# Ordering edges on VectorE for two kinds of side work in the second half: dots of the best entries' rows, and the batched heads' first selection

## The chip, the cores and the metric

The kernel runs on one core of a Trainium2 chip. The metric is device time in microseconds (us) of one launch, as the median of several runs. Each of the core's engines runs its own instructions strictly in order: TensorE (PE, matrix multiply; PEld is its weight load), VectorE (DVE), ScalarE (ACT), GpSimd (POOL), and SyncE (SP), which here only issues transfers. An instruction waits for what it reads, and all behind it on its engine wait with it.

## The reference, cut to what matters

One decoder block over 1024 tokens of width 1024: two mixers (a gated linear attention, GLA, and a chunked spatial gating) share one input projection and one output projection; then comes PEER, a mixer that retrieves, per token and head, 16 of 16384 single-neuron experts.

```python
h = modulate(rms_norm(x, norm1_w[l]), shift1, scale1)
proj = jnp.einsum('btd,de->bte', h, w_in[l])
q, k, v, r, a_lr, su, sv, g_a, g_b = jnp.split(proj, IN_SPLITS, axis=-1)
...
y = jnp.einsum('bte,ed->btd', merged, w_out[l])
x = x + gate1[:, None, :] * y
h2 = modulate(rms_norm(x, norm2_w[l]), shift2, scale2)
y2 = peer(h2, peer_w_q[l], peer_keys1[l], peer_keys2[l], peer_down[l], peer_up[l])
...
# in peer, 8 heads, K = 16: per token
v1, i1 = lax.top_k(s1, K)
v2, i2 = lax.top_k(s2, K)
cand = (v1[..., :, None] + v2[..., None, :]).reshape(B, T, H, K * K)
top_s, pos = lax.top_k(cand, K)
g = jax.nn.softmax(top_s, axis=-1).astype(h.dtype)
# per block of 128 tokens
u = expert_down[ii]
a = jax.nn.gelu(jnp.einsum('pd,ped->pe', xx, u), approximate=False)
vv = expert_up[ii]
return jnp.einsum('pe,ped->pd', gg * a, vv)
```

## The kernel before

**Halves and weights.** The tokens are worked in two halves of 512 (four blocks of 128). Each half streams 184 weight tiles of 128x512 from HBM: eight k-tiles for each of the groups V0, V1, QK0, QK1, SV0, SV1 and so on, then the output projection and PEER's query projection. `weights_ahead` (L1353) brings each tile in: a transfer on SP into `wt` (L1358, four buffers), ACT makes the high part `wh` (L1362), DVE subtracts to get the low part `wl` (L1364, four buffers each). It keeps three weights ahead of the matmuls. A buffer of `wt` is free for the next transfer once the subtract L1364 of the weight four back is done. The matmuls run as three passes, high by high, high by low, low by high (L182, L183, L185 in `mm3s`; L188 to L190 for the first or last k-tile). Their sums stand in four PSUM banks `mm`, so a group's first matmul waits until the group before has been taken out of its bank. For QK0 this is done by DVE: L1493 and L1494 make `qs` and `q1` from the first bank, again from the second, then L1510 to L1512 make `kk` and `kt` from the third and fourth. The matmuls of QK1 follow.

**Side work.** While the second half's weights stream, the PEER work of the first half's tokens runs beside it. After each k-tile `step()` lets a few generators go on; among them:

- `route` chooses the experts of a token; the heads whose best 8 candidates per side weren't enough are batched up and go through `rare` (L391): indices on DVE (L395 to L427), a gather of the scores on POOL into `qsc` (L429), then the first selection, `tops16` (L204) for both sides: MAX (L205), MAX_INDEX (L206), MATCH_REPLACE (L207), and the next eight (L208, L209), then the selection among sums (`select16`).
- `direct_rows` (L740) adds the best entry of each head for each token of blocks 0 to 3: 32 entries of 128 rows. For each, POOL gathers two tiles `uvd` of 128x1024 (L753: first the rows u of `down`, then the rows v of `up`), DVE forms the dot product of u with `h2` (L765), ACT takes Gelu (L767), DVE multiplies by the gate (L768) and adds v times the result to `yd` (L774; the first of a block is written by ACT, L770). The `uvd` tiles go round in 8 buffers that hold four entries, so an entry's gathers wait for the dot or the addition of an earlier entry. Gathers are issued one entry ahead of the dot in the text of the program.

**What sets the order.** The kernel is written as generators, but a scheduler with a model of times puts each engine's instructions in order. `tc.issue_after(x)` adds an edge to it: what stands inside may come only behind instruction `x` on the same engine. It makes no semaphore. Such edges exist before the change (Gelu behind `zlast`, `wh` and `wl` behind `hlast`). All lines in this text are those of the kernel before; in the changed kernel they stand one or two higher from L436 on.

Of the kernel before, what the change touches and what calls it, by code (L numbers as in the profile page):

```python
# [7 lines left out]
F32 = mybir.dt.float32  # L8
# [4 lines left out]
OP = mybir.AluOpType  # L13
# [68 lines left out]
def block_kernel(ctx: ExitStack, tc: tile.TileContext, x, xT, cT, w_ada, b_ada, b_adaT, n1T, w_inp, w_alr,  # L82
                 w_al, b_alT, gla_w, ln_w, ln_b, wsT, sgu_bT, w_outp, n2_w, w_qp, keysT, tab, down, up, fin_w,
                 out, dbg=None):
    nc = tc.nc
# [49 lines left out]
    sc = const.tile([P, KD], F32, name="sc")  # L135
# [68 lines left out]
    def tops16(v, ix, st):  # L204
        nc.vector.max(v[:, 0:8], st)  # L205
        nc.vector.max_index(ix[:, 0:8], v[:, 0:8], st)  # L206
        nc.vector.match_replace(st, v[:, 0:8], st, NEG)  # L207
        nc.vector.max(v[:, 8:16], st)  # L208
        nc.vector.max_index(ix[:, 8:16], v[:, 8:16], st)  # L209
# [181 lines left out]
    def rare(gi, rps):  # L391
# [25 lines left out]
        r = r2.tile([P, 4], F32, name="qr")  # L417
# [14 lines left out]
        yield  # L432
        tv = r2.tile([P, 1, 2, TOPK], F32, name="qtv")
        ti = r2.tile([P, 1, 2, TOPK], U32, name="qti")
        for c in range(2):
            tops16(tv[:, 0, c], ti[:, 0, c], sc[:, c])  # L436
        yield
        ts, sel = yield from select16(r2, tv, ti, 1, "q")
        tsel = r2.tile([P, 3 * TOPK + 2], F32, name="qtsel")
# [295 lines left out]
        while b not in done:  # L735
            qr.pump()

    zlast = []

    def direct_rows(t4, bs):  # L740
        todo = [(b, h) for b in bs for h in range(PH)]
# [16 lines left out]
        for k, (b, h) in enumerate(todo):  # L758
            lists(k + 1)
            await_routing((b // BH, h // 2), weighted)  # L760
            if h == 0:
                y = rowp.tile([P, D], F32, name="yd", tag="row")
            u, v = ents.pop(k)
            r = r2.tile([P, 2], F32, name="rdr", bufs=4)
            nc.vector.scalar_tensor_tensor(u, u, 1.0, h2s[b], op0=OP.mult, op1=OP.mult, accum_out=r[:, 0:1])  # L765
            with tc.issue_after(zlast[0]):
                nc.scalar.activation(r[:, 1:2], r[:, 0:1], AF.Gelu)  # L767
            nc.vector.tensor_tensor(r[:, 1:2], r[:, 1:2], dcol(dgtq, b, h), op=OP.mult)  # L768
            if h == 0 and YA:
                nc.scalar.activation(y, v, AF.Identity, scale=r[:, 1:2])  # L770
            elif h == 0:
                nc.vector.tensor_scalar(y, v, r[:, 1:2], None, op0=OP.mult)
            else:
                nc.vector.scalar_tensor_tensor(y, v, r[:, 1:2], y, op0=OP.mult, op1=OP.add)  # L774
            if h == PH - 1:
                nc.scalar.dma_start(y_d[b], y)
                summed.add(b)
            yield
# [275 lines left out]
    with ExitStack() as pa:  # L1054
# [299 lines left out]
        def weights_ahead(n):  # L1354
            while plan and len(made) < n:
# [5 lines left out]
                with tc.issue_after(hlast[0]):  # L1361
                    nc.scalar.activation(wh, wt, AF.Identity)  # L1362
                with tc.issue_after(hlast[1]):
                    nc.vector.tensor_tensor(wl, wt, wh.bitcast(F32), op=OP.subtract)  # L1364
                made.append((wh, wl))

        for hf in range(NHALF):
# [505 lines left out]
```

## Time and profile before

| what | us |
| --- | --- |
| runs (3) | 1446.89, 1449.89, 1451.12; median 1449.89 |
| profiled execution, own time | 1451.39 |
| its span on the core | 1449.7 |
| PE busy in the span | 1354.9 |
| DVE busy | 1091.3 |
| ACT busy | 731.4 |
| POOL busy | 282.8 |

The profiled execution's time is 1.69 us longer than its span (work around the program), and 1.5 us above the median of the runs. In the views below, times are from the start of the span. "x <- y" behind an engine's wait names what released it: an engine, a tile and a line. A row of the timeline gives the start, the duration, the engine, the line, the operation, output<-inputs with shapes, and in brackets the idle time of the engine ahead of it. An inferred releaser is the one that came last in the profile.

### The profile page before, as it was taken

What the parts mean: (1) busy time and instruction counts of PE and PEld (TensorE: products, weight loads), DVE (VectorE), ACT (ScalarE), POOL (GpSimd) and SP (SyncE); (2) the same over time, 40 slices, a digit from 0 to 9 for tenths busy, and PEclk for the clock granted to TensorE, in tenths of its full rate; (3) what the DMA queues carried; (4) which work ended last, traced back from release to release, by engine and by line L of the source; (5) the groups of instructions that cost most, each with busy time, mean ns of one, the idle gap of its engine ahead of it and who ended that gap; (6) DMA issues with size and microseconds to landing.
All of it is one profiled execution on the core that took longest, in us unless ns stands there. A gap on an engine that the chain in (4) does not pass through costs nothing.

```text
span 1449.7 us, 19609 instructions
## 1 busy us (share of the span) xinstructions
PE 1354.9 (93%) x5998; PEld 1039.5 (72%) x5998; DVE 1091.3 (75%) x3105; ACT 731.4 (50%) x1603; POOL 282.8 (20%) x276
## 2 busy tenths in 40 slices
PE   7999999999998989997989999999988999789996
PEld 5578777888887878776767777787767876445553
DVE  5784767434478669989879787777799786799775
ACT  3463333333355456465444676556656555556542
POOL 0100001000000111332342123220111033444331
PEclk9999999999999999998999999999999999999999
DMA  8753544332257575856687689796688669998984
GB/s 277 276 195 114 183 154 132 109 102 80 95 197 257 185 282 167 294 181 244 203 281 261 210 318 341 276 354 217 221 314 292 225 215 335 314 375 352 418 299 175
DMA packets 120980, 345.00 MB, mean 238 GB/s; under 512 B 15049, under 2 KB 24521, under 8 KB 108962
## 3 DMA queue, kind: packets, MB, share of 16 engines
q0 software_dynamic: 32208, 165.95, 31.5%
q1 hardware_dynamic: 71600, 133.43, 27.5%
q10 hardware_dynamic: 17058, 44.29, 8.4%
q8 instruction: 48, 0.79, 0.2%
q14 instruction: 66, 0.54, 0.1%
HBM read 319.40 MB, written 24.23 MB: 237 GB/s over the span
## 4 chain that ended last, share of the span: by engine, by line
PE 35%; DMA 10%; DVE 9%; issue 6%; ACT 5%; POOL 2%; ACTq 0%; SPq 0%; DVEq 0%; POOLq 0%
PE acc L607 6%; PE mm L182 5%; PE mm L183 5%; PE mm L185 5%; DMA uv<-in_tab_dram,ix 2%; PE mm L188 2%; PE mm L190 2%; PE mm L189 2%; PE aux L1766 1%; DMA uvd<-in_down_dram,dix 1%; PE hps L579 1%; DMA uv<-in_tab_dram,dix 1%; DVE uv L581 1%; DVE wl L1364 1%; PE hps L580 1%
## 5 line engine op out<-in xcount | busy, mean ns | idle before, releaser
L1362 ACT ACTIVATE wh<-wt 128x512 fp32r<-128x512 f32 x360 | 223.2, 628 | 306.7 <-PE mm L183 118.2
L1364 DVE TENSOR_TENSOR wl<-wt,wh 128x512 fp32r<-128x512 f32 x360 | 241.4, 683 | 142.4 <-ACT wh L1362 70.5
L182 PE MATMUL mm<-wh,hTh 128*128 128x512 f32 x648 | 257.0, 397 | 4.1 <-ACT wh L1362 4.1
L183 PE MATMUL mm<-wh,hTl 128*128 128x512 f32 x648 | 254.4, 393 | 0.0
L185 PE MATMUL mm<-wl,hTh 128*128 128x512 f32 x648 | 202.9, 396 | 0.3 <-DVE wl L1364 0.2
L182 PEld LDWEIGHTS mm<-wh,hTh 128*128 128x128 f32 x648 | 122.0, 188 | 34.0 <-ACT wh L1362 6.0
L183 PEld LDWEIGHTS mm<-wh,hTl 128*128 128x128 f32 x648 | 121.9, 188 | 26.0 <-issue 1.0
L185 PEld LDWEIGHTS mm<-wl,hTh 128*128 128x128 f32 x648 | 120.9, 188 | 27.0 <-issue 1.1
L526 POOL DMA_INDIRECT uv<-in_tab_dram,ix x73 | 77.2, 1058 | 241.2 <-ACT ix L558 145.2
L182 PE MATMUL mm<-hTh,wh 128*128 128x512 f32 x240 | 96.9, 404 | 0.0
L183 PE MATMUL mm<-hTl,wh 128*128 128x512 f32 x240 | 95.8, 399 | 0.0
L188 PE MATMUL mm<-wh,hTh 128*128 128x512 f32 x216 | 86.1, 410 | 4.0 <-ACT sg L1598 2.8
L189 PE MATMUL mm<-wl,hTh 128*128 128x512 f32 x216 | 85.7, 397 | 0.0
L581 DVE SCALAR_TENSOR_TENSOR uv<-uv,hps 128x512 f32<-128x512 f32 x110 | 73.8, 680 | 15.6 <-PE hps L580 5.7
L190 PE MATMUL mm<-wh,hTl 128*128 128x512 f32 x216 | 85.4, 396 | 0.0
L188 PE MATMUL mm<-hTh,wh 128*128 128x256 f32 (+1 forms) x208 | 70.7, 343 | 11.5 <-DVE q L1494 7.3
L185 PE MATMUL mm<-hTh,wl 128*128 128x512 f32 x240 | 71.1, 398 | 0.0
L189 PE MATMUL mm<-hTl,wh 128*128 128x256 f32 (+1 forms) x208 | 69.0, 334 | 1.8 <-DVE hTl L174 1.8
L753 POOL DMA_INDIRECT uvd<-in_down_dram,dix x32 | 36.2, 1132 | 173.2 <-DMA wt<-in_w_qp_dram 38.8
L190 PE MATMUL mm<-hTh,wl 128*128 128x256 f32 (+1 forms) x208 | 67.9, 335 | 1.7 <-DVE wl L1364 1.7
L619 DVE SCALAR_TENSOR_TENSOR vl<-uv,r,vh 128x512 fp32r<-128x512 f32 x82 | 60.0, 745 | 10.5 <-ACT vh L618 6.8
L579 PE MATMUL hps<-hh,E 128*128 128x512 f32 x132 | 62.0, 470 | 4.4 <-DVE uvu L581 2.4
(967 smaller groups left out, 2939.4 us busy)
## 6 DMA issues: line engine op xcount, KB each, us to landing
wt<-in_w_inp_dram SPq DMA_DIRECT2D x224, 256.0 KB
wt<-in_w_qp_dram SPq DMA_DIRECT2D x80, 256.0 KB
wada<-in_w_ada_dram SPq DMA_DIRECT2D x32, 512.0 KB
wt<-in_w_outp_dram SPq DMA_DIRECT2D x64, 256.0 KB
wada<-in_w_ada_dram SPq DMA_DIRECT2D x32, 256.0 KB
s_d<-so ACTq DMA_DIRECT2D x28, 256.0 KB
xr<-in_x_dram ACTq DMA_DIRECT2D x8, 512.0 KB
x_d<-x ACTq DMA_DIRECT2D x8, 512.0 KB
```

The lines of the kernel that those rows point to most:

```text
L182: nc.tensor.matmul(ps, lh, rh, start=False, stop=False)
L183: nc.tensor.matmul(ps, *((lh, rl) if feat else (ll, rh)), start=False, stop=False)
L185: nc.tensor.matmul(ps, *((ll, rh) if feat else (lh, rl)), start=False, stop=False)
L188: nc.tensor.matmul(ps, lh, rh, start=first, stop=False)
L189: nc.tensor.matmul(ps, lh, rl, start=False, stop=False)
L190: return nc.tensor.matmul(ps, ll, rh, start=False, stop=last).ins
L526: nc.gpsimd.indirect_dma_start(out=dst[:], out_offset=None, in_=src, in_offset=off)
L579: nc.tensor.matmul(hps, Ej, hh[:, sl], start=True, stop=False)
L581: nc.vector.scalar_tensor_tensor(uv[0][:, sl], uv[0][:, sl], 1.0, hps, op0=OP.mult, op1=OP.mult, accum_out=r[:, 2 + n:3 + n])
L607: ins = nc.tensor.matmul(acc[:, sl], W, v[:, sl], start=first, stop=last).ins
L1362: nc.scalar.activation(wh, wt, AF.Identity)
L1364: nc.vector.tensor_tensor(wl, wt, wh.bitcast(F32), op=OP.subtract)
```

## The change

Three places and one list. The last low-part subtract written so far is remembered in `last_wl`; the dots of `direct_rows` (L765) and the first selection of `rare` (L435, L436) get an edge behind it. No instruction is added or removed; their counts are the same on every engine, as are ACT's 68 table loads. The second group's selection (second half's tokens) comes after the last weight, where the edge says nothing.

```diff
--- before.py
+++ after.py
@@ -432,8 +432,9 @@
         yield
         tv = r2.tile([P, 1, 2, TOPK], F32, name="qtv")
         ti = r2.tile([P, 1, 2, TOPK], U32, name="qti")
-        for c in range(2):
-            tops16(tv[:, 0, c], ti[:, 0, c], sc[:, c])
+        with tc.issue_after(last_wl[0]):
+            for c in range(2):
+                tops16(tv[:, 0, c], ti[:, 0, c], sc[:, c])
         yield
         ts, sel = yield from select16(r2, tv, ti, 1, "q")
         tsel = r2.tile([P, 3 * TOPK + 2], F32, name="qtsel")
@@ -735,7 +736,7 @@
         while b not in done:
             qr.pump()
 
-    zlast = []
+    zlast, last_wl = [], []
 
     def direct_rows(t4, bs):
         todo = [(b, h) for b in bs for h in range(PH)]
@@ -762,7 +763,8 @@
                 y = rowp.tile([P, D], F32, name="yd", tag="row")
             u, v = ents.pop(k)
             r = r2.tile([P, 2], F32, name="rdr", bufs=4)
-            nc.vector.scalar_tensor_tensor(u, u, 1.0, h2s[b], op0=OP.mult, op1=OP.mult, accum_out=r[:, 0:1])
+            with tc.issue_after(last_wl[0]):
+                nc.vector.scalar_tensor_tensor(u, u, 1.0, h2s[b], op0=OP.mult, op1=OP.mult, accum_out=r[:, 0:1])
             with tc.issue_after(zlast[0]):
                 nc.scalar.activation(r[:, 1:2], r[:, 0:1], AF.Gelu)
             nc.vector.tensor_tensor(r[:, 1:2], r[:, 1:2], dcol(dgtq, b, h), op=OP.mult)
@@ -1361,7 +1363,7 @@
                 with tc.issue_after(hlast[0]):
                     nc.scalar.activation(wh, wt, AF.Identity)
                 with tc.issue_after(hlast[1]):
-                    nc.vector.tensor_tensor(wl, wt, wh.bitcast(F32), op=OP.subtract)
+                    last_wl[:] = [nc.vector.tensor_tensor(wl, wt, wh.bitcast(F32), op=OP.subtract).ins]
                 made.append((wh, wl))
 
         for hf in range(NHALF):
```

What it does to the order: the first nine dots of `direct_rows` stand 4 to 19 weights later than before on DVE (the first behind the 181st subtract L1364 in place of the 163rd, the ninth behind the 194th in place of the 189th); the tenth to the fifteenth stand where they were or one or two weights later, and from the sixteenth on the places are the same, counted so. On POOL the two MEMSETs of `smask` move ahead of the gathers of two entries, and the gather of `qsc` moves behind one more gather of `up`. PE's order is the same up to the end of QK1 but for one set of matmuls; further on, the second half's matmuls and PEER's accumulations are interleaved differently in many places.

The first place is DVE at the end of QK0 of the second half, where `qsc` is first read. `wl_5937` is the low part of QK1's first weight (the 201st subtract L1364), `uvd_5898` and the `yd` rows belong to the direct entries. Before:

```order
L774 SCALAR_TENSOR_TENSOR yd_5736<-uvd_5734,rdr_5769,yd_5736 128x1024
L425 CAST qr_5532<-rtok0_127 128x1
L768 TENSOR_TENSOR rdr_5929<-rdr_5929,dgt0_2_141 128x1
L205 MAX qtv_5573<-qsc_5544 128x8 x2
L1364 TENSOR_TENSOR wl_5937<-wt_5934,wh_5936 128x512
L774 SCALAR_TENSOR_TENSOR yd_5736<-uvd_5767,rdr_5857,yd_5736 128x1024
L427 TENSOR_SCALAR rcol0_129<-qr_5532 128x1 x4
```

The changed kernel at the same weight:

```order
L767 SCALAR_TENSOR_TENSOR uvd_5898,rdr_5929<-uvd_5898,h2d_5674 128x1024
L424 TENSOR_SCALAR rtok0_127<-qix_5536 128x1
L1366 TENSOR_TENSOR wl_5937<-wt_5934,wh_5936 128x512
L776 SCALAR_TENSOR_TENSOR yd_5736<-uvd_5734,rdr_5769,yd_5736 128x1024
L770 TENSOR_TENSOR rdr_5902<-rdr_5902,dgt0_1_140 128x1
L425 CAST qr_5532<-rtok0_127 128x1
L770 TENSOR_TENSOR rdr_5929<-rdr_5929,dgt0_2_141 128x1
L776 SCALAR_TENSOR_TENSOR yd_5736<-uvd_5767,rdr_5857,yd_5736 128x1024
L427 TENSOR_SCALAR rcol0_129<-qr_5532 128x1 x4
```

The MAX on `qsc` no longer stands ahead of the weight's low part, and neither does the first `yd`, which is now behind it; the dot of entry 12 (`uvd_5898`), which stood ahead of the 200th weight's low part, stands behind that one and directly ahead of this one.

The second place is DVE directly behind it: the next weight's low part `wl_5955` (the 202nd), and the rows that empty QK0's banks (L1493 to L1512 before; `qs`, `q1`, `kk`, `kt`). Before:

```order
L206 MAX_INDEX qti_5574<-qtv_5573,qsc_5544 128x8
L765 SCALAR_TENSOR_TENSOR uvd_5925,rdr_5974<-uvd_5925,h2d_5674 128x1024
L206 MAX_INDEX qti_5574<-qtv_5573,qsc_5544 128x8
L226 TENSOR_TENSOR candq_5585<-qtv_5573 128x24
L226 TENSOR_TENSOR candq_5585<-qtv_5573 128x16
L1364 TENSOR_TENSOR wl_5955<-wt_5952,wh_5954 128x512
L774 SCALAR_TENSOR_TENSOR yd_5736<-uvd_5855,rdr_5902,yd_5736 128x1024
L207 MATCH_REPLACE qsc_5544<-qtv_5573,qsc_5544 128x128
L765 SCALAR_TENSOR_TENSOR uvd_5970,rdr_6001<-uvd_5970,h2d_5674 128x1024
L1493 SCALAR_TENSOR_TENSOR qs_6008<-mm_5798,eG_6006 128x4x64
L1494 SCALAR_TENSOR_TENSOR q1_6009<-mm_5798,eG_6006 128x256
L1493 SCALAR_TENSOR_TENSOR qs_6015<-mm_5799,eG_6013 128x4x64
```

The changed kernel:

```order
L1366 TENSOR_TENSOR wl_5955<-wt_5952,wh_5954 128x512
L767 SCALAR_TENSOR_TENSOR uvd_5925,rdr_5974<-uvd_5925,h2d_5674 128x1024
L1495 SCALAR_TENSOR_TENSOR qs_6008<-mm_5798,eG_6006 128x4x64
L1496 SCALAR_TENSOR_TENSOR q1_6009<-mm_5798,eG_6006 128x256
L776 SCALAR_TENSOR_TENSOR yd_5736<-uvd_5855,rdr_5902,yd_5736 128x1024
L1495 SCALAR_TENSOR_TENSOR qs_6015<-mm_5799,eG_6013 128x4x64
L1496 SCALAR_TENSOR_TENSOR q1_6016<-mm_5799,eG_6013 128x256
L1512 TENSOR_TENSOR kk_6020<-mm_5800,eGi_6024 128x4x2x64
L1513 TENSOR_TENSOR kk_6020<-mm_5800,dt_6022 128x4x64
L1514 TENSOR_TENSOR kt_6021<-mm_5800,dt_6022 128x4x64
L205 MAX qtv_5573<-qsc_5544 128x8 x2
L1366 TENSOR_TENSOR wl_5982<-wt_5979,wh_5981 128x512
```

The two MAX_INDEX, the two sums `candq`, one MATCH_REPLACE and one dot (`uvd_5970`) that stood ahead of the first `qs` are now behind the third bank's `kt`; one `yd` now stands between the first bank and the second.

The third place is ACT some 15 us earlier, at `eG`, `eGi` and `dt` (the decays of QK0) and the high parts `wh_5824` (the 197th weight) and `wh_5864`. Before:

```order
L1488 ACTIVATE eG_6006<-G0_5435 128x512
L1488 ACTIVATE eG_6013<-G1_5443 128x512
L770 ACTIVATE yd_5736<-uvd_5678,rdr_5737 128x1024
L1552 ACTIVATE egl3_5795<-G3_5459 128x4x2
L1507 ACTIVATE eGi_6024<-G0_5435 128x512
L1508 ACTIVATE dt_6022<-dt_6022 128x512
L1508 ACTIVATE dt_6033<-dt_6033 128x512
L1362 ACTIVATE wh_5824<-wt_5822 128x512
L1362 ACTIVATE wh_5864<-wt_5862 128x512
```

The changed kernel:

```order
L1490 ACTIVATE eG_6006<-G0_5435 128x512
L1490 ACTIVATE eG_6013<-G1_5443 128x512
L769 ACT_TABLE_LOAD
L769 ACTIVATE rdr_5737<-rdr_5737 128x1
L1554 ACT_TABLE_LOAD
L1554 ACTIVATE egl3_5795<-G3_5459 128x4x2
L1509 ACTIVATE eGi_6024<-G0_5435 128x512
L1510 ACTIVATE dt_6022<-dt_6022 128x512
L1364 ACTIVATE wh_5824<-wt_5822 128x512
L1510 ACTIVATE dt_6033<-dt_6033 128x512
L772 ACTIVATE yd_5736<-uvd_5678,rdr_5737 128x1024
L1364 ACTIVATE wh_5864<-wt_5862 128x512
```

The Gelu of entry 8 (`rdr_5737`), which stood higher with three others, is now between two table loads of its own ahead of `egl3`, and `yd_5736`, the first of a block, moves behind `wh_5824`.

## The prediction

> **What bounds the kernel now.** The page's first part says which engine to follow:
>
> ```profile
> PE 1354.9 (93%) x5998; PEld 1039.5 (72%) x5998; DVE 1091.3 (75%) x3105; ACT 731.4 (50%) x1603; POOL 282.8 (20%) x276
> ```
>
> PE is busy for 93% of the span, so DVE's order is worth only what it adds to or takes from PE's gaps. The dots run from 518 to 763 us (the group of their line gives 32 of them, quoted below), so next come the windows of that stretch. A row has the engines' busy us in the order PE, PEld, DVE, ACT, POOL, then the granted clock, the DMA share and GB/s.
>
> ```profile
> 550.00:575.00 25.00, 25.00 (x125) 20.20 (x124) 24.70 (x101) 16.33 (x29) 1.00 (x1) 1.00 0.37 126
> 575.00:600.00 25.00, 25.00 (x126) 20.71 (x125) 25.00 (x136) 13.06 (x23) 7.88 (x8) 1.00 0.72 232
> 600.00:625.00 25.00, 25.00 (x107) 17.95 (x106) 17.62 (x54) 13.46 (x23) 8.12 (x8) 1.00 0.75 268
> 650.00:675.00 25.00, 17.74 (x79) 14.43 (x78) 23.70 (x64) 12.28 (x21) 5.96 (x5) 0.80 0.74 265
> 725.00:750.00 25.00, 19.75 (x85) 15.89 (x84) 16.57 (x30) 9.06 (x26) 11.06 (x11) 0.86 0.92 325
> ```
>
> From 550 to 600 DVE is full, but PE is full too: nothing is to be won there. From 600 to 625 DVE has 7.4 us to spare. PE loses time in two windows, 7.3 us after 650 and 5.3 us after 725, both with a lower clock. PE's waits, asked for in 640 to 680 and in 725 to 760, give one row each (line waited for: us in total, times, longest):
>
> ```profile
> PE mm L188 <- DVE q L1494: 7.3, 1, 7.3
> PE gaux L1537 <- DVE rdr L768: 5.3, 1, 5.3
> ```
>
> The first is the change's target: QK1's first matmul waits for QK0's first bank. The timeline shows what DVE did ahead of it:
>
> ```profile
> 640.45 1.27 DVE L774 SCALAR_TENSOR_TENSOR yd<-uvd,rdr,yd 128x1024 f32<-128x1024 f32 x1
> 641.65 0.68 DVE L1364 TENSOR_TENSOR wl<-wt,wh 128x512 fp32r<-128x512 f32 x1
> ...
> 651.30 0.49 DVE L205 MAX8 qtv<-qsc 128x8 f32<-128x128 f32 x2 [3.26 <-DMA qsc<-s_d,qix]
> 651.79 0.69 DVE L1364 TENSOR_TENSOR wl<-wt,wh 128x512 fp32r<-128x512 f32 x1
> ...
> 653.84 0.08 DVE L206 MATCH_VALUE_LOAD qti<-qtv,qsc 128x8 f32 x1
> ...
> 654.11 1.21 DVE L765 SCALAR_TENSOR_TENSOR uvd<-uvd,h2d 128x1024 f32<-128x1024 f32 x1
> 655.24 0.08 DVE L765 DVE_READ_ACCUMULATOR uvd<-uvd,h2d 128x1 f32 x1
> ...
> 655.68 0.68 DVE L1364 TENSOR_TENSOR wl<-wt,wh 128x512 fp32r<-128x512 f32 x1
> 656.29 1.28 DVE L774 SCALAR_TENSOR_TENSOR yd<-uvd,rdr,yd 128x1024 f32<-128x1024 f32 x1
> 657.48 0.08 DVE L207 MATCH_VALUE_LOAD qsc<-qtv,qsc 128x8 f32 x1
> ...
> 657.75 1.21 DVE L765 SCALAR_TENSOR_TENSOR uvd<-uvd,h2d 128x1024 f32<-128x1024 f32 x1
> 658.89 0.42 DVE L1493 SCALAR_TENSOR_TENSOR qs<-mm,eG 128x256 f32<-128x256 f32 x1
> 659.22 0.41 DVE L1494 SCALAR_TENSOR_TENSOR q<-mm,eG 128x256 f32<-128x256 f32 x1
> ```
>
> DVE stood idle for 3.26 us at MAX, and then had 7.6 us of work (651.30 to 658.89) ahead of the first `qs`, while PE had run out. But the idle time is not MAX's alone: the weight behind it was late too, as ACT, SP and PE show.
>
> ```profile
> 642.35 14.38 SPq L1358 DMA_DIRECT2D wt<-in_w_inp_dram  x6
> 651.13 0.63 ACT L1362 ACTIVATE wh<-wt 128x512 fp32r<-128x512 f32 x1 [4.85 <-DMA wt<-in_w_inp_dram]
> 652.13 0.39 PE L190 MATMUL mm<-hTh,wl 128*128 128x512 f32 x1
> 659.78 0.77 PE L188 MATMUL mm<-hTh,wh 128*128 128x512 f32 x1 [7.26 <-DVE q L1494]
> ```
>
> The transfer of weight 201 was issued at 642.35, as soon as the subtract at 641.65 had freed its buffer, and landed 8.8 us later; its high part was ready at 651.76, its subtract could not start before 651.8. So **taking MAX out of the way frees no 3.26 us**: in the changed order that subtract still stands ahead of the banks, and DVE waits there for ACT instead.
>
> **The change part by part.**
>
> *Taken from ahead of the first bank* (second place in the order): by differences of starts, the first MAX_INDEX 0.27 us (653.84 to 654.11), the second with both sums 0.44 (655.24 to 655.68), MATCH_REPLACE 0.27 (657.48 to 657.75), one dot 1.14 (657.75 to 658.89): 2.12 us. The two `yd` ahead of the bank stay two, since one comes from above the subtract and one goes below. Two products L768 and a CAST are added, three rows of 1 column. Nearest row for one:
>
> ```profile
> L768 DVE TENSOR_TENSOR rdr<-rdr,dgt 128x1 f32<-128x1 f32 x4 | 0.6, 146 | 0.0
> ```
>
> Starts follow each other closer than that (four in 0.3 us), so 0.2 us for the three. Net **1.9 us** earlier.
>
> *The start of that piece.* Weight 201 is issued when weight 197's subtract (641.65) is done. In the changed order one `yd`, 1.20 us by its starts (640.45 to 641.65), has moved behind that subtract, and there are as many dots ahead of it. Against that, weight 197's high part comes later on ACT, for a Gelu between two table loads has been put in front of it and a `yd` and a `dt` taken out:
>
> ```profile
> 635.09 1.14 ACT L770 ACTIVATE yd<-uvd,rdr 128x1024 f32<-128x1024 f32 x1
> ...
> 636.75 1.14 ACT L1508 ACTIVATE dt<-dt 128x512 f32<-128x512 f32 x2
> 637.80 1.66 ACT L1362 ACTIVATE wh<-wt 128x512 fp32r<-128x512 f32 x3
> 639.48 1.28 ACT L767 ACT_TABLE_LOAD   x1
> ```
>
> That is two loads, 2.56 us, and some 0.2 for the Gelu, less 1.14 and half of the two `dt`, 0.57: +1.05 us. The high part would start at 638.9 and be done near 639.5, still ahead of 640.45, where its subtract would come. So weight 201 would be issued and land up to 1.2 us earlier. But the dot of entry 12 now stands directly ahead of its subtract, and its gather is late: it used to wait for a `yd` of DVE (issue 638.37, row below), and has its buffer now from the `yd` on ACT that moved behind weight 197's high part, which by the rows above ends near 641.5. The gathers' own landings bound it:
>
> ```profile
> 638.37 1.67 POOL L753 DMA_INDIRECT uvd<-in_down_dram,dix  x1 [0.65 <-DVE yd L774]
> 701.52 5.88 DMA uvd<-in_down_dram,dix
> 642.84 8.44 DMA qsc<-s_d,qix
> ```
>
> From 641.9 this is 647.8 to 650.3; with the dot's 1.2 us the subtract starts between 650.6 (weight 201 bounds) and 651.5 against 651.79. I take 0.6 us.
>
> *Behind the first bank* a `yd` (1.20) now stands ahead of the second one. Before, the second bank was taken out 0.66 us after the first (two rows, 0.33 apart by 658.89 and 659.22); it is now 1.9 us. PE needs it about 1.3 us after its first matmul at the clock there (three matmuls, 0.43 apart by the rows below), so I charge 0.3 us, between 0 and 1.2.
>
> *The clock.* What the pause does to the clock:
>
> ```profile
> 641.70 0.39 PE L183 MATMUL mm<-hTl,wh 128*128 128x512 f32 x1
> 641.93 0.39 PE L182 MATMUL mm<-hTh,wh 128*128 128x512 f32 x1
> ...
> 664.19 0.63 PE L190 MATMUL mm<-hTh,wl 128*128 128x512 f32 x1
> 664.61 0.50 PE L182 MATMUL mm<-hTh,wh 128*128 128x512 f32 x1
> ```
>
> Matmuls start 0.23 us apart before the pause and 0.43 behind it; the 11 from 659.78 to 664.61 take 4.83 us in place of 2.5. So the pause costs 2.3 us more than its length. A pause of 7.26 - 2.2 = 5.1 us, nearly that of the second one (5.3, and its window's clock fell to 0.86), keeps this cost. The Trainium skill ("TensorE: Matmul & The Clock Gate", Part 1) has the rate halved after one idle window of about 3.4 us, the windows running freely; both pauses here agree with it. By that rule the 2.3 us would go for certain below 3.4 us, and a pause of 5.1 us might or might not hold a whole window: the sum would be 2.3 us lower where it doesn't.
>
> *The early dots* (nine, 4 to 19 weights later) cost as much as before:
>
> ```profile
> L765 DVE SCALAR_TENSOR_TENSOR uvd<-uvd,h2d x32: 1206/1216/1277, 518.0 to 763.1; 128x1024 f32<-128x1024 f32 x32
> ```
>
> Nine are 11 us. They leave the full windows up to 600, and up to six of them fit into the 7.4 us that DVE has free from 600 to 625, beside a PE that is full in all three windows. I cost this at nothing. Without that cover a dot too many there would cost PE its 1.2 us.
>
> *The rest of the stream.* From entry 16 on the order counted in weights is the same, and so are the rows at the second pause (a `yd` that waits for its gather, a dot, then what PE needs). It is paced by gathers that wait for dots and additions; these move with the weights. I leave the 5.3 us as they are; bounds 0 and twice that. The later interleaving of PEER with the matmuls differs in many places. The longest waits of PE there:
>
> ```profile
> PE mm L182 <- ACT wh L1362: 3.4, 4, 2.0
> PE acc L626 <- DVE fin L700: 2.4, 1, 2.4
> ```
>
> One such wait more or less is 2.4 us; I take 0, bounds -3 and +3.
>
> **Sum:** -1.9 - 0.6 + 0.3 = -2.2 us. Against the profiled execution's own 1451.39 us that is 1449.2; the runs' median is 1.5 us below that execution, and against it the sum gives **1447.7 us**.
>
> **The rivals.**
>
> A. *The whole pause goes.* If DVE comes to the first bank when QK0's last matmul ends (652.5), 7.3 us and the clock's 2.3 go: -9.6 us, 1440.3. For it: `qsc` is the row's named releaser. Against it: the weight's own high part was 0.46 us later than the MAX. Half way, the second pause shrinks as the stream comes earlier (its wait is on a gather): -2.2 - 2.6 and some clock, -5 to -7, 1443 to 1445.
>
> B. *The wait changes its name only.* If the gather of entry 12 lands at the late end and the second bank costs its full 1.2 us, -1.9 + 0.3 + 1.2 is about 0: 1449.5. For it: `wt` 201's 8.8 us and the gather share the same DMA queues, 0.74 busy in that window.
>
> C. *Slower.* The early dots, now later, hold their buffers longer, so the stream has an entry less of look-ahead. A gather issued less than its landing time (5.9 to 8.4 us) ahead of its dot or `yd` stops DVE, and the weights' subtracts behind it stop PE: that is what the second pause is. It decides when a gather is issued less than about 7 us ahead of its place, between 630 and 735. One more pause of that kind costs 5.3 us and 2.3 for the clock: +7.6 - 2.2 = +5.4, 1455.3. For it: a gather 3.5 us later for entry 12. Against it: from entry 16 on nothing moves. The Trainium skill ("DMA: Bandwidth & Descriptors", Anatomy of one DMA) fits a transfer that GpSimd issues by 2.0 us and its bytes at 436 KB a us, by which 512 KB take an estimated 3.2; the trace has 5.88 or more, so the trace decides, and by the page's figure C could not happen.
>
> **How the numbers follow.** A change under 0.3% (4.35 us) cannot be told from none in this kernel. Forecast (-4 to 0, with the late bounds -6 to +3): 0.45. A in full or half: 0.25. B: 0.12. C, with a bad late interleaving: 0.18. Faster by over 0.3%: A's 0.25 and 0.08 of the forecast, 0.33. Slower: C's 0.18 and 0.02 of B, 0.20. Within: 0.47. The range reaches from A in full to the edge of C: 1440 to 1455.
>
> **What would show it.** DVE's wait in 626 to 660 should name `wh` in place of `qsc`, with about 3 us; PE's wait on L1494 should be near 5 us, and the clock's low stretch should stay. The sum fails if that wait is under 3.5 us (A), if it is still 7 (B), or if PE has a wait on a `yd` or a dot between 600 and 735 that has no row above (C). The second pause at its old length would confirm that the stream only moved along.

## The result, and the profile after

| | before | after |
| --- | --- | --- |
| median of 20 runs each, same chip, us | 1447.12 | 1455.05 |
| lowest and highest, us | 1439.15, 1452.36 | 1446.41, 1461.81 |
| ratio, 95% interval | | 1.0060 [1.0044, 1.0076] |
| profiled execution, its span, us | 1451.39, 1449.7 | 1457.38, 1455.7 |

The changed kernel is slower by 0.6%, 7.9 us by the medians; 1447.7 had been predicted. The page's first part says that PE's work is the same and its idle time is not (engine, busy us, share, count):

```profile
PE 1354.6 (93%) x5998; PEld 1043.0 (72%) x5998; DVE 1092.3 (75%) x3105; ACT 730.1 (50%) x1603; POOL 300.8 (21%) x276
```

1354.6 of 1455.7 us, where it was 1354.9 of 1449.7: the 6 us between these two executions are PE's waiting. PE's waits in the stretch of the dots, 535 to 790 us of after (line waited for: us in total, times, longest), beside 7.3, 5.3, nothing and 1.3 in before:

```profile
PE mm L188 <- DVE q L1496: 5.8, 1, 5.8
PE gaux L1539 <- DVE rdr L770: 4.5, 1, 4.5
PE aux L278 <- DVE cnt L275: 2.5, 1, 2.5
PE mm L188 <- ACT vt L1426: 2.2, 1, 2.2
```

The pause at QK0's first bank became shorter, as forecast, and two waits grew in its place (a `ktok` wait of 1.0 went). Nothing here is worth 8 us. What DVE does ahead of the bank, in the timeline of after (start, duration, engine, line, operation, idle time ahead in brackets):

```profile
650.95 1.22 DVE L767 SCALAR_TENSOR_TENSOR uvd<-uvd,h2d 128x1024 f32<-128x1024 f32 x1 [3.48 <-issue]
...
652.16 0.68 DVE L1366 TENSOR_TENSOR wl<-wt,wh 128x512 fp32r<-128x512 f32 x1
...
657.62 0.42 DVE L1495 SCALAR_TENSOR_TENSOR qs<-mm,eG 128x256 f32<-128x256 f32 x1
...
659.48 0.41 DVE L1495 SCALAR_TENSOR_TENSOR qs<-mm,eG 128x256 f32<-128x256 f32 x1
```

DVE no longer waits at MAX, but at the dot of entry 12 (L767): its gathered rows are late, the last of them landing at 650.87. From weight 201's subtract to the first `qs` it takes 5.46 us, where it took 7.10 (651.79 to 658.89). The matmuls of after behind the pause:

```profile
658.51 0.76 PE L188 MATMUL mm<-hTh,wh 128*128 128x512 f32 x1 [5.83 <-DVE q L1496]
659.08 0.63 PE L189 MATMUL mm<-hTl,wh 128*128 128x512 f32 x1
...
664.20 0.50 PE L185 MATMUL mm<-hTh,wl 128*128 128x512 f32 x1
```

They start 0.43 us apart up to 664.20: the stretch at half rate stayed. The new lost time stands much later. The largest waits of PE between about 905 and 1130 us, first of before, then of after:

```profile
PE mm L182 <- ACT wh L1362: 3.4, 4, 2.0
PE acc L626 <- DVE fin L700: 2.4, 1, 2.4
```

```profile
PE sps L1619 <- ACT us L1418: 5.0, 1, 5.0
PE tps L550 <- DVE uv L582: 3.7, 3, 1.8
```

These are PEER entries of the second half's interleaving, and a wait of 5 us, some 180 us behind the last dot, that before did not have.

### The profile page after: what moved, and what is told of

It reads as the page before. It is cut to its first block, busy times and chain, and to the rows that moved or that the text cites. A ratio compares the mean times of both kernels' runs of the same rounds, so it can differ in the third digit from the quotient of the medians.

```text
span 1455.7 us, 19622 instructions
## 1 busy us (share of the span) xinstructions
PE 1354.6 (93%) x5998; PEld 1043.0 (72%) x5998; DVE 1092.3 (75%) x3105; ACT 730.1 (50%) x1603; POOL 300.8 (21%) x276
## 4 chain that ended last, share of the span: by engine, by line
PE 31%; DMA 9%; DVE 8%; issue 5%; ACT 3%; POOL 1%; ACTq 0%; DVEq 0%; POOLq 0%
PE acc L608 6%; PE mm L182 4%; PE mm L183 4%; PE mm L185 4%; DMA uvd<-in_down_dram,dix 2%; DMA uv<-in_tab_dram,ix 2%; PE mm L188 2%; PE mm L189 2%; DMA uv<-in_tab_dram,dix 2%; PE mm L190 2%; PE hps L580 2%; DMA wt<-in_w_outp_dram 1%; PE hps L581 1%; DVE uv L582 1%; PE acc L628 1%
## 5 line engine op out<-in xcount | busy, mean ns | idle before, releaser
L1364 ACT ACTIVATE wh<-wt 128x512 fp32r<-128x512 f32 x360 | 222.6, 627 | 309.4 <-PE mm L183 118.9
L754 POOL DMA_INDIRECT uvd<-in_down_dram,dix x32 | 39.6, 1237 | 138.4 <-DMA wt<-in_w_qp_dram 38.2
```

## The experiments

Each ratio is to the kernel before on the same chip, with its 95% interval. "The late part" is everything from about 800 us on; the orders of the two kernels hold the same instructions up to there on each engine, so that they can be put together. In most kernels a given order was held, by edges that make no semaphore, from each instruction to the next on its engine:

```diff
         block_kernel(tc, *args)
+        made = {i.name: i for i in nc.cur_bb.bb.instructions}
+        for names in held_orders():
+            held = [f"I-{n}" for n in names if f"I-{n}" in made]
+            for a, b in zip(held, held[1:]):
+                tc.add_manual_dep(made[b], a, ..., reason="held order")
```

Lines in e1, e2, e4 and e10 are those of the changed kernel, in the others those of before. One thing is seen from the orders without a run: the edge on the selection by itself leaves every engine's order as before, and the edge on the dots by itself gives the changed kernel's order on every engine. So the whole change is the dots' edge.

**e1 to e4: where the time is.** e1 is the changed kernel again; e2 has its order up to about 800 us and before's from there, e3 the other way round; e4 is the change with the edge left off the first twelve entries.

```diff
 # e2: held from 800 us on, in the changed kernel
+    late order of before
 # e3: held from 800 us on, in the kernel before
+    late order of the changed kernel
 # e4
-            with tc.issue_after(last_wl[0]):
+            with tc.issue_after(last_wl[0]) if k >= 12 else nullcontext():
```

> The changed kernel once more, beside the next three on one chip. Both theories: 5 to 10 us slower than before (ratio 1.004 to 1.007).

> The changed kernel up to about 800 us of the span, and from there on every engine held in the order of before. Theory 'late' (the loss comes from the other interleaving of PEER's accumulations and the weights' matmuls after 800 us): the loss goes, 2 us faster to 1 us slower than before, 7 to 10 us faster than the changed kernel. Theory 'stream' (the direct entries, with less look-ahead, cost more waits between 500 and 800 us than the pause at QK0 gains): still 5 to 9 us slower than before.

> The reverse: the kernel before up to about 800 us, and from there on every engine held in the order of the changed kernel. Theory 'late': 6 to 10 us slower than before, like the changed kernel. Theory 'stream': within 2 us of before.

> The edge on the dots of entries 12 to 31 only, none on the first twelve: the early dots stay where they were, the last one ahead of QK0's first bank moves behind it, MAX stays ahead of the subtract, and from about 830 us on the order is that of before. Theory 'late': PE's pause at QK0 is 1 to 2.5 us shorter than in before, the kernel 0 to 2.5 us faster. Theory 'stream': no loss here either, since the early dots keep their look-ahead: within 2 us of before.

Measured: e1 1.0057 [1.0033, 1.0081], e2 1.0002 [0.9975, 1.0030], e3 1.0056 [1.0032, 1.0080], e4 0.9971 [0.9942, 0.9999]. The loss is in the late order, all of it that can be seen, and the two effects of e2 and e3 add up to e1's. The early part of the change shows no gain (e2's interval goes from 3.6 us faster to 4.3 slower, so it does not exclude the 2.2 us that were forecast). Why so little, when the pause is shorter? These are PE's waits from 535 to 790 us, e3 (early order of before), then e2 (early order of the change):

```profile
PE mm L188 <- DVE q L1494: 7.5, 1, 7.5
PE gaux L1537 <- DVE rdr L768: 4.5, 1, 4.5
PE mm L188 <- ACT vt L1424: 1.3, 1, 1.3
PE aux L1535 <- ACT ktok L1523: 1.0, 1, 1.0
```

```profile
PE mm L188 <- DVE q L1496: 4.7, 1, 4.7
PE gaux L1539 <- DVE rdr L770: 4.3, 1, 4.3
PE aux L278 <- DVE cnt L275: 2.6, 1, 2.6
PE mm L188 <- ACT vt L1426: 2.2, 1, 2.2
```

In total 14.3 against 13.8 us. 2.8 are won at the pause; 2.6 are paid at L278, PE's small product that needs the counts `cnt`, the end of the selection chain on DVE. That row stands, e3 first:

```profile
678.27 0.15 DVE L275 COPY cnt<-incq 128x1 f32<-128x1 f32 x1
```

```profile
684.95 0.14 DVE L275 COPY cnt<-incq 128x1 f32<-128x1 f32 x1
```

It comes 6.7 us later, with PE's row at the same place among the weights. The late part in one row for each, for the same matmuls (window, its length, busy us of PE, PEld, DVE, ACT, POOL, clock, DMA share, GB/s), e3 and then e2:

```profile
906.50:1127.90 221.40, 198.44 (x928) 158.75 (x929) 182.25 (x438) 125.82 (x278) 38.93 (x37) 0.96 0.79 278
```

```profile
907.00:1115.00 208.00, 196.35 (x924) 158.56 (x923) 179.43 (x424) 125.74 (x271) 34.14 (x35) 0.96 0.79 282
```

They are 13 us apart in these two executions, with the same clock and the same DMA share: waits of PE, not a slower chip.

**e5, e6: is it one stretch?** e3 with the new late order only from 808 to 975 us, and only from 975 us on; the rest as before.

```diff
 # e5
+    808 to 975 us: order of the changed kernel; else before's
 # e6
+    from 975 us on: order of the changed kernel; else before's
```

> Before's order everywhere but from about 808 to 975 us of the span, where every engine is held in the order of the changed kernel. From the profiles of the four runs before this one, PE needs 166.5 us for that stretch in either order (the new wait on the gated units' evacuation is paid back inside it). Theory 'one stretch': within 2 us of before. Theory 'everywhere' (the new interleaving costs something in each part): 2 to 5 us slower.

> Before's order up to about 975 us, the changed kernel's from there to the end. Theory 'one stretch' (the loss is between 975 and 1126 us, where PE took 157 to 160 us in the new order against 147 to 150): 7 to 10 us slower than before. Theory 'everywhere': 3 to 5 us slower.

Measured: e5 1.0036 [1.0010, 1.0062], e6 1.0053 [1.0025, 1.0081]. Neither is free. Together they are more than e3, by 0.3%, which is not clear of the noise; whether the seam at 975 us makes waits of its own is not shown. So cutting the order in time does not split the loss. e6 comes up again below.

**e7: is it ACT's line at the bank?** In e3, ACT's evacuation `us` (L1416), for which PE waits 3.5 us near 940 us, stands behind the gate `r` of a PEER entry (L589, L591), which waits for DVE. e7 is e3 with one `us` ahead of them.

```diff
 ACT
-L1416 ACTIVATE us<-mm
-L589 ACTIVATE r<-r
-L591 ACTIVATE r<-r
-L1416 ACTIVATE us<-mm
+L1416 ACTIVATE us<-mm x2
+L589 ACTIVATE r<-r
+L591 ACTIVATE r<-r
```

> The kernel with the old order up to 800 us and the new one behind it, and one exchange on ACT: an evacuation of the gated units (us) moves ahead of two small operations of a PEER entry (r), which waited for a gathered row while PE waited for the bank. Theory 'line behind a gather': PE's wait of 3.5 to 5 us near 940 falls under 1.5 us; the time falls by 2 to 4 us against the same kernel without the exchange (so 4 to 7 us slower than before), unless the entry itself is what PE needs next: then PE waits there instead and the time stays at 8 us slower.

Measured: 1.0024 [0.9999, 1.0049], that is 0 to 7 us slower than before, nearer to the first branch of the forecast (4 to 7) than to the second (8). But its profile shows the second: PE waits at the same place, now for the entry itself (PE from 906 to 1128 us, then DVE from 925 to 965). The fall against e3, which ran on another chip, is not clear of the noise.

```profile
PE acc L626 <- ACT vh L618: 6.5, 5, 4.8
```

```profile
DVE uv L586 <- issue: 6.0, 1, 6.0
```

**e12: does PE come too early?** e7, and on PE the four accumulations of that entry behind 20 more of the weights' matmuls.

```diff
 PE
-L626, L627, L626, L627 MATMUL acc<-vh|vl,e_8414
 L1617 MATMUL sps<-svg,wst
 ...
 L185 MATMUL mm<-wl,hTh
+L626, L627, L626, L627 MATMUL acc<-vh|vl,e_8414
```

> As e7 (the late order of the changed kernel, us of the bank ahead of r on ACT), and on PE the four accumulations of the entry for which e7 waited 4.83 us at 943.69 stand behind the sps matmuls and 20 more of the weights' matmuls, some 8 us later by PE's own time. If the late loss is that PE meets PEER's products before they are there ('too early'): the wait of 4.8 us on acc<-vh goes and leaves less than 1.5 us in 935 to 960; the waits of PE between 906 and 1128 fall by about 4 us, and the ratio to before comes near 1.000 (e7: 1.0024). If DVE itself is late ('the supply is late': DVE stands idle for 6.0 us at the gathered row L586 and the weights' low parts are queued behind it), PE finds another name to wait for within some 10 us, a weight's low part or sps, the sum of its waits in 906 to 1128 falls by less than 1.5 us, and the ratio stays at 1.002 or above. The rows before 900 us are those of before, so their waits should be as in e3 and e7.

Measured: 1.0071 [1.0046, 1.0097], and PE found another name, two more `us` that stand on ACT behind the same `r`:

```profile
PE sps L1617 <- ACT us L1416: 6.1, 1, 6.1
```

```profile
DVE uv L586 <- issue: 5.7, 1, 5.7
```

Its waits from 906 to 1128 us add up to 20.9 us, e7's to 21.1. So moving ACT's or PE's rows only gives the wait another name: what is late is the row in DVE's line, the product of a gathered row, L586. Everything behind it on DVE waits along, `r` on ACT behind DVE, and PE behind both.

**e13 to e18: what makes that row late.** The PEER entries' gathers go into a ring of tiles `uv` (L519), and a finished block's rows `fin` are worked in a tile of the same ring until SP has stored them (L712). The semaphores of the gather in question, `uv_8408`, and its neighbours on POOL (DMASW: POOL's own transfers; DMAHW: those of SP and ACT), before and after:

```
L526 DMA uv_8408<-in_tab_dram,ix_8406 128x2048 [waits DMASW7_49,DVE_49]
L526 DMA uv_8497<-in_tab_dram,ix_8495 128x2048 [waits DMAHW4_49,DMAHW2_49,PE_49]
```

```
L527 DMA uv_8408<-in_tab_dram,ix_8406 128x2048 [waits DMAHW3_49,DVE_49,DMAHW4_49,PE_49,Activation_49]
...
L527 DMA uv_8497<-in_tab_dram,ix_8495 128x2048 [waits DMASW7_49,DVE_49]
```

In before, `uv_8408` takes the buffer of an earlier entry and the next gather takes `fin`'s; in the changed kernel they are swapped, because one `vl` of the earlier entry (L619, its last use) stands behind the next entry's dot on DVE in place of ahead of it. e13 is e3 with that `vl` put ahead again, which swaps the buffers back; e14 moves the same `vl` less far, which leaves `fin`'s buffer; e15 is before's order with the `vl` moved behind the dot, which gives it the bad buffer. (The buffers are read from the semaphores of each program.) e16, e17 and e18 are e3, e13 and e14 once more, on one chip.

```diff
 DVE, e13
 L619 vl_8373<-uv_8238
 L1364 wl_8812
+L619 vl_8377<-uv_8238
 L731 E, L570 e2, L1364 wl_8844
 L586 uv_8317<-uv_8317,hr_8319
-L619 vl_8377<-uv_8238
 DVE, e14
 L731 E, L570 e2, L1364 wl_8844
+L619 vl_8377<-uv_8238
 L586 uv_8317<-uv_8317,hr_8319
-L619 vl_8377<-uv_8238
 ACT, e13 and e14
 L1362 wh_8793
+L618 vh_8376<-uv_8238
 L558 ix, L1362 wh_8811, L1362 wh_8843
-L618 vh_8376<-uv_8238
 DVE, e15 (order of before)
-L619 vl_8377<-uv_8238
 L570 e2
 L586 uv_8317<-uv_8317,hr_8319
+L619 vl_8377<-uv_8238
```

> As e3 (before's order up to about 800 us, the changed kernel's from there), with one vl of an entry (L619, the second of uv_8238) five places earlier on DVE, ahead of the next entry's dot, and its vh on ACT four places earlier. The buffers of uv are handed out in the order in which they come free, so the gather of the entry after next (uv_8408, the one whose dot stands at 938.44 in e3 behind 4.87 us of idle DVE) takes the buffer that this vl frees, and no longer the one of the block's result fin, which is free only when its store to HBM has landed; that one goes to the gather behind. Theory 'one buffer': this gather is issued some 6 us earlier (931.3 in e3, about 925 as in e2); DVE's idle time ahead of that dot falls from 4.9 to 6.1 us to under 3.5, the wait of PE for us or acc behind it (3.5 to 6.1) goes to under 1.5, and the ratio to before falls from e3's 1.0056 to between 1.001 and 1.003. Rival 'many small waits': the late loss is spread over the PEER entries, this one place gives back less than 2 us, ratio 1.004 to 1.006.

> Control of e13: the same vl one place earlier than in e3 (directly ahead of the next dot), its vh as in e13, and the gather still in the buffer of fin. Theory 'one buffer': the idle time at the dot of uv_8408 stays at 4.5 us or more and the ratio at 1.004 to 1.007, as e3. If the place of the vl itself mattered (it stands ahead of a dot that waits for its gather), it would be like e13.

> The order of before throughout, held, but that same vl two places later, directly behind the next entry's dot; this alone makes the gather of uv_8408 take the buffer of fin, as in the changed kernel. Theory 'one buffer': DVE's idle time at that dot grows by 2 us or more against before (2.4 to 2.8 there at the entry that now takes fin's buffer) and the ratio comes to 1.002 to 1.004. Rival 'many small waits': 0.999 to 1.0015.

> e3 again, on the chip of e17 and e18: 1.004 to 1.007 if the late order's loss is as large on every chip; near 1.002 if e13 and e14 came out low because of the chip or of their runs of before (1447.1 there, 1443.8 in e3's).

> e13 again. Theory 'one buffer' (most of the late loss is the one late gather): at least 3 us faster than e16 and e18 on the same chip, ratio 1.000 to 1.0025. Rival 'many small waits': within 2 us of e16 and e18.

> e14 again, the control with fin's buffer: within 2 us of e16 and at least 3 us slower than e17 by 'one buffer'; if it lies with e17 and both are below e16, it was the place of the vl and its vh, not the buffer, that gave back time.

| kernel | gather uv_8408 takes | ratio |
| --- | --- | --- |
| e3, e16 | fin's buffer | 1.0056 [1.0032, 1.0080], 1.0054 [1.0032, 1.0077] |
| e14, e18 | fin's buffer | 1.0015 [0.9989, 1.0042], 1.0058 [1.0030, 1.0086] |
| e13, e17 | the entry's | 1.0008 [0.9982, 1.0034], 1.0001 [0.9974, 1.0028] |
| e15 | fin's buffer, else before's order | 1.0012 [0.9986, 1.0038] |

On one chip, the medians of e16, e17 and e18 are 1453.27, 1445.25 and 1451.43 us, before's 1444.53: moving one row of 0.75 us ahead of one dot (with its `vh` on ACT) gives back 8.0 us, as much as the whole loss, while moving it almost as far without the buffer gives back 1.8. The executions show where. The same two of the weights' subtracts, ahead of the place and behind it, in e16 and then in e17:

```profile
925.98 0.69 DVE L1364 TENSOR_TENSOR wl<-wt,wh 128x512 fp32r<-128x512 f32 x1 [0.37 <-ACT wh L1362]
...
962.58 0.69 DVE L1364 TENSOR_TENSOR wl<-wt,wh 128x512 fp32r<-128x512 f32 x1
```

```profile
924.63 0.69 DVE L1364 TENSOR_TENSOR wl<-wt,wh 128x512 fp32r<-128x512 f32 x1 [0.37 <-ACT wh L1362]
...
954.72 0.68 DVE L1364 TENSOR_TENSOR wl<-wt,wh 128x512 fp32r<-128x512 f32 x1
```

That is 36.6 against 30.1 us. With `fin`'s buffer the same stretch takes 34.7 us in e3, 35.8 in e14, 36.4 in e18 and 36.1 in the changed kernel's profile; with the entry's, 29.9 in e13. So 5 to 7 us are lost at this place in each execution; where the rest of the 8 is lost was not located. The chain in the timeline of e16, from the store of `fin` to PE:

```profile
927.94 0.35 SPq L712 DMA_DIRECT2D out_dram<-fin  x1
...
936.12 0.98 POOL L526 DMA_INDIRECT uv<-in_tab_dram,ix  x1 [9.85 <-DMA wt<-in_w_inp_dram]
...
944.68 1.22 DVE L586 SCALAR_TENSOR_TENSOR uv<-uv,hr 128x1024 f32<-128x1024 f32 x1 [6.28 <-issue]
...
945.95 0.20 ACT L589 ACTIVATE r<-r 128x1 f32<-128x1 f32 x1 [6.48 <-DVE uv L586]
...
946.38 0.58 ACT L1416 ACTIVATE us<-mm 128x512 f32<-128x512 f32 x1
...
947.01 2.07 PE L1617 MATMUL sps<-svg,wst 128*128 128x128 f32 x8 [4.92 <-ACT us L1416]
```

The gather goes out 8.2 us after the store was issued and its row is used 8.6 us after that. (The profile names another releaser of POOL in each execution, a weight's transfer here, `jk` in e3, a matmul in e18: a sign that none of them is it. The trace's records of the semaphores show that it is the store: its last landing is at 935.23 in e16, 930.40 in e3 and 934.49 in e15, and the gather goes 0.9 us behind it each time. The gather's last landing in e16 is at 944.59, and the row starts at 944.68. That it is the buffer is what e13 and e17 show.) The same rows in e17:

```profile
927.70 0.75 DVE L619 SCALAR_TENSOR_TENSOR vl<-uv,r,vh 128x512 fp32r<-128x512 f32 x1
...
929.23 1.07 POOL L526 DMA_INDIRECT uv<-in_tab_dram,ix  x1 [4.32 <-ACT ea L730]
...
938.28 1.22 DVE L586 SCALAR_TENSOR_TENSOR uv<-uv,hr 128x1024 f32<-128x1024 f32 x1
```

The gather leaves 0.8 us after the `vl` is through, and has landed (937.94) when DVE comes to its row. PE shows no wait from 900 to 960 us; DVE's longest wait there, 2.7 us, is for a weight's high part. The store of `fin` was issued at 926.58 there, so this gather stands 2.7 us behind it in place of 8.2. PE in the ten microseconds of the wait, e16 and then e17 (same columns as above):

```profile
940.00:950.00 10.00, 5.08 (x25) 4.50 (x24) 4.72 (x14) 3.99 (x11) 2.00 (x3) 0.72 0.96 374
```

```profile
940.00:950.00 10.00, 9.99 (x61) 8.73 (x62) 9.10 (x32) 6.00 (x16) 3.13 (x4) 1.00 1.03 402
```

25 matmul records against 61, and the clock at 0.72. e15 shows the wait coming with the buffer in before's order, too:

```profile
944.42 1.23 DVE L586 SCALAR_TENSOR_TENSOR uv<-uv,hr 128x1024 f32<-128x1024 f32 x1 [6.70 <-issue]
...
947.02 0.51 PE L626 MATMUL acc<-vh,e 128*128 128x512 f32 x1 [2.76 <-ACT vh L618]
```

There it costs PE only 2.8 us, and the time, 1.0012, cannot be told from before's; 1.002 to 1.004 had been expected, and the number lies with the rival. In before's order no `us` stands behind that entry's `r`. That the price depends on what stands behind the late row would explain it, but was not tested.

Two more results do not fit smoothly. e14 came out at 1.0015 on the first chip, where 1.004 to 1.007 had been expected, though its profile has the wait (5.2 us at L586, 3.8 of PE) and the long stretch; the same kernel as e18 gave 1.0058, and the intervals overlap. And e6, whose gather of `uv_8408` has the good buffer, still measured 1.0053. Its profiled execution (1445.26) is among its four fastest of 1445 to 1458 and shows no large wait. So an order can lose as much in another way, and what e6's slower executions lose stays open.

**e8, e9: what the first pause is made of.** The selection's move is only a by-product; does it alone help the pause? e8 is before's order with nine rows of DVE (eight of the selection, and the dot ahead of the bank) behind the third bank's `kt`. e9 goes further: 47 rows reordered so that all QK0's banks are emptied first, `yd`, dots and selection behind them, and one Gelu on ACT further down.

```diff
 DVE, e8
-L205 MAX x2, L206 MAX_INDEX x2, L226 candq x2, L207 MATCH_REPLACE, L765 dot
 L1493 qs, L1494 q, ... L1512 kt
+L205 MAX x2, L206 MAX_INDEX x2, L226 candq x2, L207 MATCH_REPLACE x2, L765 dot
 DVE, e9
+L1364 wl, L1493 qs, L1494 q, L1493 qs, L1494 q, L1364 wl, L1510 kk, L1511 kk, L1512 kt
 ... yd, dots, selection
```

> Before's order on every engine and everywhere, but nine rows of DVE at QK0's end: the first selection and one dot move behind the third bank's kt. The effect that the change was said to have, alone. Theory 'given back at the count' (in the changed kernel the selection ends 6.7 us later, and PE waits 2.5 us for its count at L278): here the selection is only 2 us late, so PE does not wait at L278, the pause at QK0 is about 2 us shorter (5.3 in place of 7.4) and the kernel 1.5 to 4 us faster. Rival 'stream' (whatever is gained at the pause is lost at the next wait on a gather, near 737 us): that wait grows by 2 us and the kernel is within 1 us of before.

> Before's order but for 47 rows of DVE at QK0's end and one Gelu on ACT: behind the first weight of QK1, DVE empties the first three banks at once, then come weights, dots, additions and the selection; the Gelu of the dot that is now later moves behind the next table load, so that the fourth bank's exponential is not held up. Theory 'line at DVE' (the pause is DVE's order and not the weight's arrival): the pause falls from 7.4 to 1 to 2 us and the half clock behind it (2.3 us) goes; PE waits 1 to 3 us for the next weights instead; 3 to 6 us faster than before. Rival 'stream': the direct entries come 2 to 3 us later against PE, the wait near 737 us grows from 4.5 to 8 or more, and the kernel is 0 to 2 us faster.

Measured: e8 0.9983 [0.9957, 1.0009], e9 1.0010 [0.9988, 1.0031]. Neither is told from before, and e9 missed both of its forecasts, 3 to 6 and 0 to 2 us faster. In e8 the pause falls from 7.3 in before to 5.2, there is no wait at L278 (`cnt` comes 31.3 us behind weight 201's subtract, 30.6 in before, 38.3 in e2), and a new one of 1.7 appears at the fourth bank (620 to 775 us):

```profile
PE mm L188 <- DVE q L1494: 5.2, 1, 5.2
PE gaux L1537 <- DVE rdr L768: 2.5, 1, 2.5
PE mm L188 <- DVE kt L1512: 1.7, 1, 1.7
```

In e9 the pause is gone, and PE waits for parts of the weights instead (640 to 700 us, then the window of the old pause):

```profile
PE mm L182 <- ACT wh L1362: 4.1, 2, 2.9
PE mm L185 <- DVE wl L1364: 1.2, 1, 1.2
PE mm L188 <- DVE q L1494: 1.0, 1, 1.0
PE mm L188 <- DVE kt L1512: 1.0, 1, 1.0
```

```profile
650.00:675.00 25.00, 17.82 (x84) 13.63 (x82) 21.09 (x59) 11.14 (x19) 6.69 (x6) 1.00 0.70 248
```

PE is busy for 17.8 of the 25 us, as in before (17.7), and the way from one weight's subtract to the same later one takes 218.0 us in e9 (568.5 to 786.5) and 217.6 in e3 (562.9 to 780.5). So emptying the banks gives back nothing by itself. The first wait for a high part, 1.23 us, is for a weight's transfer. The longest, 2.90 up to 675.15, is not: ACT makes that high part at 674.49, behind the exponentials that follow a Gelu which had waited for a dot of DVE:

```profile
670.97 0.20 ACT L767 ACTIVATE rdr<-rdr 128x1 f32<-128x1 f32 x1 [4.80 <-DVE uvd L765]
```

That is e9's own order, and whether the banks first and the weights in time would gain something was not tested.

The clock stays at 1.00 in that window of e9, whose waits up to 680 us are 1.03, 1.23, 1.16, 1.01 and 2.90 long. But there is no length below which it always stays. In before, half rate follows the wait of 2.4 us for `fin` that ends near 917 (columns as above):

```profile
917.50:920.70 3.20, 3.20 (x13) 2.81 (x13) 3.17 (x7) 1.78 (x4) 0.00 (x0) 0.50 0.46 175
```

Between 500 and 1260 us of the twenty traces, a stretch at half rate begins within, or no later than 1.5 us behind, all 70 waits of PE of 3.4 us or more, and 27 of the 44 of 1.9 to 3.4. (The Trainium skill, "TensorE: Matmul & The Clock Gate", Part 1, halves the rate after an idle window of about 3.4 us; the traces agree for the waits of 3.4 us or more, and for the shorter ones the measurement decides.)

**e10, e11: two controls.** e4 again, and before's own order held by the edges.

```diff
 # e10: as e4
 # e11
+    order of before, held
```

> The edge on the dots of entries 12 to 31 once more. If the first result (ratio 0.997) was the effect: 2 to 5 us faster again. If it was chance: within 2 us of before.

> The kernel before, with its own order held by edges on every engine from about 500 us on: a control of the tool that the other runs use. 1.000 within 0.25%.

Measured: e10 0.9987 [0.9961, 1.0012], e11 1.0007 [0.9981, 1.0034]. Holding an order costs nothing that can be seen. e4's gain did not come back clearly; the two together lie near 0.998. No version here is shown to be faster than before.

## Why the prediction was wrong, point by point

1. **The failed step: "The later interleaving ... I take 0, bounds -3 and +3."** It measured +8 (e3, e16). One buffer of PEER's gathers went from an entry to the finished block's rows; the wait at that place is 3.5 (e3), 4.9 (e16) or 5.8 us (e18) of PE, with half rate behind it, and the stretch around it takes 6.5 us longer in e16 than in e17. I had priced it from the largest single wait in that part of before (2.4 us), but the price of a reordered part is not the largest wait that the old order had: the new order can have one that the old order did not.
2. **Taken from ahead of the first bank, -1.9 us: right.** From weight 201's subtract to `qs`, 7.10 became 5.46 us, -1.6; in e1 and e2 the pause came to 4.6 and 4.7 us, where 5.1 had been forecast (5.8 in the profile after).
3. **The start of the piece, -0.6 us: of no use in the profiled execution.** The subtract started at 652.16 in place of 651.79 (+0.4; 0.7 outside the bound), since the gather of entry 12 landed at 650.87 and not between 647.8 and 650.3. DVE's wait there did not take the name `wh`, but that of the dot, 3.5 us. As the text had it, no 3.26 us came free.
4. **Second bank and early dots: as costed; half clock: stayed, but not by the rule quoted.** The second bank was taken out 1.9 us after the first (657.62, 659.48), as forecast, and PE has no wait there. From 550 to 600 PE is full in all kernels. The half-rate stretch stayed even at a pause of 4.7 us; but below 3.4 us it would not have gone "for certain", as before's own wait of 2.4 us for `fin` shows. With its half rate that wait cost more than the 2.4 us at which the later interleaving was priced.
5. **What was left out of the early sum: the end of the selection chain.** The rows of the selection were counted only as gone from ahead of the bank, and what waits for them got no term. MAX moved from just ahead of weight 201's subtract (651.30) to behind the third bank (661.40), `cnt` at its end came 6.7 us later, and PE has a row that waits for it, 2.5 us at L278; `vt` took another 0.9, `ktok` gave 1.0 back. With them PE's waits in the early part are 0.5 us shorter in e2 than in e3, in place of the 2.2 us. e8, whose `cnt` keeps its place to within 0.7 us, has no such wait. The rows behind the ones that move, down to the next one that PE reads, belonged in the sum.
6. **The rivals.** C had the sign and nearly the time (1455.3), but by luck, with the wrong mechanism: the direct entries' stream lost no look-ahead that cost anything, the second pause stayed at 4.3 to 4.5 us, and e2 with the whole early order is not seen to be slower. It was, though, a gather issued too late that stopped DVE and then PE, as in C, only of PEER's ring and 300 us on. A (the whole pause goes) was answered by e9: the pause can go without any time going. B's late gather came true (650.87, beyond its late end), but the second bank cost nothing, and B had no later loss. The weights' transfers and the gathers do not share a queue, as B has it: the trace lists them on two (q1, q0), and what it shows as 0.74 busy are the 16 DMA engines.

## What to carry to other kernels

An ordering edge in a scheduled program is priced by what it does to the whole order and to the buffers: compare the order and the semaphores on every engine to the end of the program, and look first for a gather or transfer whose buffer now comes from something slow to free, such as a tile that is stored to memory. When the wait of the engine that bounds the kernel changes its name but not its length as things are moved (e7, e12), look for the late row on another engine; and where a pause vanishes without the time vanishing (e9), look for what the engine waits for in its place. A ring shared by tiles of different lifetimes can make a reordering cost time far behind its place, by which tile takes which buffer; a buffer of its own for the stored tile would be the thing to try, which was not done here.

## What the runs showed of the hardware that was not expected

The length of the half-rate stretch does not follow the length of the pause: some 14 matmuls behind 5.83 us in after, 13 behind 4.71 in e2, 11 behind 7.26 in before. Part of the stretch can lie in the pause itself, as before's does, 5 of its 10.2 us (columns as above):

```profile
654.70:659.80 5.10, 0.02 (x1) 0.05 (x1) 5.10 (x15) 2.13 (x5) 2.13 (x2) 0.50 1.03 401
```

In the twenty traces every stretch at half rate is 3.4 us long or a multiple of that, up to 17.1 (the one at the end of each trace, which has no end on record, left out). Single executions of one kernel differ by far more than the effects here (20 runs of after: 1446.4 to 1461.8), so the times of two single executions could not have told 8 us from none; the same two subtracts around one place could, 34.7 to 36.6 us against 29.9 and 30.1. And a gather of 128x2048 floats near 940 us, with the DMA share at 0.96, took 8.5 us from its issue to its last landing (e16), about as long as the 8.2 us between the store's issue and the gather's.
